# The output projection in seven half-size products, with its sums made on chip

## The chip, the cores and the metric

The kernel runs on one core of a Trainium2 chip. The metric is device time in microseconds (us) of one execution, from the first to the last instruction and what lies around them. The engines are TensorE (PE for its matmuls, PEld for its weight loads), VectorE (DVE), ScalarE (ACT), GpSimd (POOL) and SyncE (SP, whose queue issues all DMAs here). They run side by side, each through its own list of instructions in order, and wait for each other by semaphores.

## The reference

A decoder layer with two attention mixers, A (block-sparse) and B (compressed, selected and windowed), over 512 tokens of 1024 channels. What follows the attention is what the change touches:

```python
y_a = o_a * jax.nn.silu(z_a)
y_b = o_b * jax.nn.silu(z_b)
g_m = jax.nn.sigmoid(gate_m)
merged = g_m[..., :D_MODEL] * (y_a @ w_branch_a[l]) + g_m[..., D_MODEL:] * (y_b @ w_branch_b[l])
x = x + merged @ w_out[l]
```

`gate_m` is a part of `rms_norm(x) @ w_in`; everything is float32.

## The kernel before

**Precision.** PE multiplies a rounded format, so every operand is split into a high half (a cast) and a low half (the operand minus its high half). A product is three matmuls: high x high, low x high, high x low (`mm3`, L416). For weights the raw tile `wr` comes from memory, `wh` (L337, mostly ACT, sometimes POOL) and `wl` (L341, mostly DVE) are its halves; `NW` = 8 of each are kept, and `NRAW` = 5 raw tiles.

**Stages.** First the projections, with the attention woven between them on PE; then the gates of mixer A (`gmgate`, tile `pgc`); then the eight branch products of A (`branch(0, j)`, tile `pbr`, 12 matmuls of 512 columns each); then, for j = 0 to 3, the gates of B for channel tiles j and j + 4 together (`gate_pair`, tile `pgw`) and the branch products `branch(1, j)` and `branch(1, j + 4)`; then the output (`last`, tile `po`).

**Gate pairs in seven products.** A pair of gate tiles is a 2 x 2 block product (two halves of the tokens, two channel tiles, two halves of the 8 k tiles). `gate_pair` makes it from seven products of half size instead of eight (Winograd's form of Strassen's scheme), each of 12 matmuls of 256 columns. It needs sums of the weights (`ws`, L378, made on the way in: `s1 = a21 + a22`, `s2 = s1 - a11`, `s4 = a12 - s2`, `s3 = a11 - a21`) and sums of the inputs, made once for all pairs in `x_again` (rows `xa`, `ta`, `tb`, `T`, `th`, `hl`). The products run in the order 1, 5, 6, 3, 7, 2, 4 and use two banks of PSUM pool `g`; sums over products are made by ACT copies (`cu`, `c5`) and DVE additions (L1352 to L1364).

**Merging.** When a branch product is done, DVE multiplies it with its gate (L1382, "gm<-gm,pbr"), adds mixer A's part (L1447, "gm<-gm,gm"), ACT casts the high half `mh` (L1450), DVE or POOL makes the low half `ml` (L1451).

**Output.** Four column groups of 256, in each four row tiles of 128 tokens; every `po` tile is 8 k x 3 = 24 matmuls of 256 columns: 384 in all. An eviction on DVE (L1552) adds a `po` tile to the input rows `xr`, and SP writes it.

**What sets the order.** A planner in the kernel walks the work with its own estimates of durations and writes each engine's list; what stands here are its lists. Tiles named `gm`, `mh`, `ml`, `xa` and the like share `NATT` = 40 attention buffers; a tile that takes the slot of an older one waits until that was last read. PSUM banks: 2 `g`, 2 `s`, 3 `t`, 1 `o`; `s`, `t` and `o` are the attention's.

A path for the output in seven products is in the kernel (`WOUT`, `last_wino`, `m_sums`), and is not used.

Of the kernel before, what the change touches and what calls it, by code (L numbers as in the profile page):

```python
# [19 lines left out]
D = 1024  # L20
# [69 lines left out]
def hybrid_kernel(ctx: ExitStack, tc: tile.TileContext, x, x0, xT, wtok, wchan, gains, w1,  # L90
# [1185 lines left out]
    def x_again():  # L1276
# [4 lines left out]
        T3 = [alloc("T", "T3", dt=F32R) for _ in range(2)]  # L1281
        pools = [alloc("ph", "T1", dt=F32R) for _ in range(3)] + [sp.tile([P, S], F32R, name=nm("T2"), tag="pl", bufs=3) for _ in range(3)]
        for k in range(4):
# [16 lines left out]
            c.do(either(256), lambda e, x1=x1, x2=x2, tb=tb: e.tensor_sub(tb[:, h[0]], x2[:, h[1]], x1[:, h[1]]))  # L1300
            c.do(either(256), lambda e, x2=x2, ta=ta, tb=tb: e.tensor_sub(tb[:, h[1]], x2[:, h[0]], ta[:, h[1]]))
            for n_, (hi, lo) in enumerate((dst[0][0], dst[0][1])):
# [3 lines left out]
                TX[n_ + 1, k] = hi, lo, None  # L1306
            hi, lo = hl_[1], hl_[2]
            c.do({"A": ca(512)}, lambda e, tb=tb, hi=hi: e.copy(hi, tb))
            c.do(either(512), lambda e, tb=tb, hi=hi, lo=lo: e.tensor_sub(lo, tb, hi.bitcast(F32)))
            for n_ in range(2):  # L1310
                TX[n_ + 3, k] = hi[:, h[n_]], lo[:, h[n_]], None
            c.mark(("T", k))
            c2.call(lambda c=c, c1=c1, c2=c2: c.start(max(c1.t, c2.t)))

    def gate_pair(w, j):
        t1, t2 = att("gm", F32), att("gm", F32)
        yield need(*(("T", k) for k in range(4)))
# [25 lines left out]
        c1 = act("a", "c1", h[0])  # L1343
        yield from run(5, "b", True)
# [7 lines left out]
        c12 = Chain(now[0] + 230).do({"D": cd(256)}, lambda e: e.tensor_add(t1[:, h[1]], b["u2"], ps["b"][:, :256]), lambda: ps["b"])  # L1352
# [3 lines left out]
        yield c12.ready  # L1356
        yield from run(2, "c", True)
        c = Chain(now[0] + 230).do({"D": cd(256)}, lambda e: e.tensor_add(t1[:, h[0]], b["c1"], ps["c"][:, :256]),
                                   lambda: ps["c"]).call(lambda: release(b["u"], c.t))
        c.do(either(512), lambda e: e.tensor_mul(t1, t1, R))  # L1360
        gms[w, j] = t1, c.do({"A": ca(512)}, lambda e: e.activation(t1, t1, AF.Tanh, scale=0.5))
# [3 lines left out]
        d.do(either(256), lambda e: e.tensor_mul(t2[:, h[1]], t2[:, h[1]], R[:, h[1]]))  # L1365
        gms[w, j + 4] = t2, d.do({"A": ca(512)}, lambda e: e.activation(t2, t2, AF.Tanh, scale=0.5))

    def branch(w, j):
# [6 lines left out]
        for c in mm3(ps, ws, [yhl["ab"[w], k] for k in range(4)]):  # L1375
# [5 lines left out]
        yield gc.ready  # L1381
        return Chain(max(now[0] + 230, gc.t)).do({"D": 602}, lambda e: e.scalar_tensor_tensor(  # L1382
            g, g, 1.0, ps, op0=ALU.add, op1=ALU.mult), ps)
# [16 lines left out]
    def gemms():  # L1400
# [32 lines left out]
        for j in (0, 4, 1, 5, 2, 6, 3, 7):  # L1433
            if not WGATES:
                yield from gmgate(1, j)
            elif j < 4:
                yield from gate_pair(1, j)
# [7 lines left out]
            ch = yield from branch(1, j)  # L1445
            g0, g1, a, b = gms[0, j][0], gms[1, j][0], att("mh"), att("ml")
            ch.do(either(512), lambda e, g0=g0, g1=g1: e.tensor_add(g0, g0, g1))  # L1447
            fs[j] = g0, ch.mark(("m", j))
            w_ = 256 if WOUT and j < 4 else 512
            ch.do({"A": ca(w_)}, lambda e, g0=g0, a=a, w_=w_: e.copy(a[:, :w_], g0[:, :w_]))  # L1450
            ch.do(either(w_), lambda e, g0=g0, a=a, b=b, w_=w_: e.tensor_sub(b[:, :w_], g0[:, :w_], a[:, :w_].bitcast(F32)))  # L1451
            ms[j] = a, b, ch
            if WOUT and j >= 4:
                m_sums(j - 4, fs)
# [28 lines left out]
    def last_wino(ms, xr):  # L1483
# [26 lines left out]
        rest = ((5, "b", True), (6, "a", False), (3, "b", False), (7, "a", False), (2, "c", True), (4, "a", False))  # L1510
        for c, p_, z_, first in [(c, 1, "a", True) for c in range(2)] + [(c, *z) for c in range(2) for z in rest]:
            ws = W.take(2, 256)
            for t in range(2):
# [156 lines left out]
```

## Time and profile before

| | us |
|---|---|
| median of 3 runs | 480.58 (480.02 to 481.2) |
| the profiled execution | 479.89 |
| its span, first to last instruction | 478.1 |

The granted TensorE clock is 1.0 throughout. Some lines of the profile are shown in the prediction. There L416 is `mm3`'s line, so matmuls are told apart by their tile. A group's mean duration of a matmul (281 ns for 256 columns) is longer than the distance between two of them, since matmuls overlap in the array.

### The profile page before, as it was taken

How to read it: one execution, taken by the hardware profiler on the slowest of the kernel's cores; microseconds unless marked ns; L12 is line 12 of the kernel's file. 1: busy time of each engine (PE TensorE's matmuls, PEld its weight loads, DVE VectorE, ACT ScalarE, POOL GpSimd, SP SyncE). 2: the span in 40 equal slices, each digit the busy share in tenths (PEclk: the TensorE clock that was granted, in tenths of full speed). 3: DMA queues.
4: the chain of work that ended last, by engine and by line, in shares of the span. 5: the costliest groups of instructions: out<-in, count | busy, mean ns of one | idle time of the engine just before them, and what ended most of it. 6: DMA issues, size and time to landing. Idle time of an engine off the chain costs nothing.

```text
span 478.1 us, 9136 instructions
## 1 busy us (share of the span) xinstructions
PE 468.5 (98%) x3220; PEld 429.2 (90%) x3220; DVE 368.2 (77%) x920; ACT 282.5 (59%) x683; POOL 166.9 (35%) x218
## 2 busy tenths in 40 slices
PE   9999999999999999999999999999989999999997
PEld 8999898999999989888888888888868899889997
DVE  6888988788898489897778768786698789875331
ACT  8666594587787276677776568676654455533200
POOL 1266492077764033554442045346031101100000
PEclk9999999999999999999999999999999999999999
DMA  8835234443433313222212222211821243285421
GB/s 303 239 101 155 69 108 114 136 134 114 110 102 119 111 45 111 54 60 68 63 47 72 83 67 66 69 44 48 275 59 61 90 133 106 59 257 185 145 67 44
DMA packets 29053, 51.30 MB, mean 107 GB/s; under 512 B 3216, under 2 KB 5648, under 8 KB 29008
## 3 DMA queue, kind: packets, MB, share of 16 engines
q1 hardware_dynamic: 29008, 50.73, 35.5%
q8 instruction: 25, 0.41, 0.4%
q14 instruction: 20, 0.16, 0.1%
HBM read 47.96 MB, written 2.75 MB: 106 GB/s over the span
## 4 chain that ended last, share of the span: by engine, by line
PE 82%; DVE 10%; ACT 3%; issue 2%; DMA 2%; SPq 0%; ACTq 0%; DVEq 0%
PE pgc L416 21%; PE pgt L416 18%; PE po L416 9%; PE pgw L416 7%; PE O L1035 6%; PE pt L1001 5%; PE sps L954 3%; PE sps L955 3%; PE pbr L416 3%; DVE wl L341 3%; PE pq L886 2%; DVE ws L378 1%; ACT wh L337 1%; DVE gm L1382 1%; ACT xa L1288 1%
## 5 line engine op out<-in xcount | busy, mean ns | idle before, releaser
L341 DVE TENSOR_TENSOR wl<-wr,wh 128x512 fp32r<-128x512 f32 (+1 forms) x113 | 79.1, 704 | 5.6 <-ACT wh L337 5.1
L416 PE MATMUL pgt<-wh,hh 128*128 128x256 f32 (+1 forms) x288 | 82.6, 287 | 0.4 <-DVE X L772 0.4
L416 PE MATMUL pgt<-wl,hh 128*128 128x256 f32 (+1 forms) x288 | 81.6, 283 | 0.2 <-DVE wl L341 0.2
L416 PE MATMUL pgt<-wh,hl 128*128 128x256 f32 (+1 forms) x288 | 81.1, 281 | 0.0
L337 ACT CAST wh<-wr 128x512 fp32r<-128x512 f32 (+1 forms) x94 | 57.2, 619 | 18.2 <-DMA wr<-in_wout 12.9
L992 POOL TENSOR_SCALAR P<-P,sst,gate 128x512 f32<-128x512 f32 (+3 forms) x56 | 40.2, 722 | 62.7 <-DVE sst L991 58.5
L973 DVE CUSTOM_DVE_ANT_0 sb<-sps,T 128x512 f32<-128x512 f32 (+3 forms) x96 | 46.0, 485 | 20.0 <-PE sps L955 18.5
L416 PE MATMUL pgc<-hh,wh 128*128 128x512 f32 x144 | 59.5, 414 | 0.0
L416 PE MATMUL pgc<-hl,wh 128*128 128x512 f32 x144 | 56.8, 395 | 0.0
L416 PE MATMUL pgc<-hh,wl 128*128 128x512 f32 x144 | 56.8, 394 | 0.0
L988 ACT ACTIVATE P<-sb,sst 128x512 f32<-128x512 f32 (+3 forms) x88 | 50.9, 579 | 8.0 <-DVE sst L973 7.3
L416 PEld LDWEIGHTS pgt<-wh,hh 128*128 128x128 f32 x288 | 54.3, 188 | 1.2 <-PE sps L955 0.6
L416 PEld LDWEIGHTS pgt<-wl,hh 128*128 128x128 f32 x288 | 54.2, 188 | 0.6 <-DVE wl L341 0.4
L416 PEld LDWEIGHTS pgt<-wh,hl 128*128 128x128 f32 x288 | 54.3, 188 | 0.4
L1013 ACT CAST ph<-pt 128x512 fp32r<-128x512 f32 (+2 forms) x72 | 33.5, 479 | 26.5 <-PE pt L1001 25.9
L1001 PE MATMUL pt<-cst,P 128*128 128x128 f32 x232 | 40.6, 272 | 0.0
L1015 DVE TENSOR_TENSOR pl<-pt,ph 128x512 fp32r<-128x512 f32 (+2 forms) x72 | 38.5, 549 | 2.0 <-ACT ph L1013 1.7
L458 POOL TENSOR_TENSOR nr<-nss,mhalf 128x4 f32<-128x4 f32 x28 | 30.7, 1099 | 16.3 <-DVE nss L457 15.8
L416 PE MATMUL po<-wh,mh 128*128 128x256 f32 x128 | 36.0, 281 | 0.2 <-DVE xr L1552 0.2
L416 PE MATMUL po<-wh,ml 128*128 128x256 f32 x128 | 35.9, 281 | 0.2 <-DVE ml L1451 0.2
L416 PE MATMUL po<-wl,mh 128*128 128x256 f32 x128 | 35.9, 280 | 0.0
L992 POOL TENSOR_SCALAR P<-P,sst 128x512 f32<-128x512 f32 (+3 forms) x32 | 21.6, 679 | 32.9 <-DVE sst L991 31.8
(266 smaller groups left out, 1270.4 us busy)
## 6 DMA issues: line engine op xcount, KB each, us to landing
wr<-in_wchan SPq DMA_DIRECT2D x52, 256.0 KB, 2.8
wr<-in_wtok SPq DMA_DIRECT2D x36, 256.0 KB, 2.9
T<-rtab SPq DMA_DIRECT2D x16, 256.0 KB, 3.8
wr<-in_w SPq DMA_DIRECT2D x16, 256.0 KB, 2.8
wr<-in_wbr SPq DMA_DIRECT2D x16, 256.0 KB, 2.7
wr<-in_wout SPq DMA_DIRECT2D x16, 256.0 KB, 3.0
xr<-in_x SPq DMA_DIRECT2D x8, 256.0 KB, 5.4
out_y<-xr SPq DMA_DIRECT2D x16, 128.0 KB, 1.7
```

Of the source, the lines that this page charges most:

```text
L337: e.copy(hi, raw())
L341: c.do(either(n), lambda e: e.tensor_sub(lo, raw(), hi.bitcast(F32))).mark((w, 1, i))
L416: nc.tensor.matmul(dst, sts[i][a], mvs[i][b], start=(start and i == a == b == 0), stop=(stop and i == n - 1 and b == 1), skip_group_check= ...
L458: c.do({"p": 430 + 150 * w}, lambda e: e.tensor_tensor(v(dst), v(ss), mhalf[:parts, :w], op=ALU.pow))
L954: nc.tensor.matmul(sps[:, :n], qs[:, b * P:(b + 1) * P], ks[:, :n], start=True, stop=False)
L973: e.tensor_tensor_reduce(z["sb"][:, :L], sps[:, :L], T[:, S - L:], scale=-1.0, scalar=3e38, op0=ALU.add, op1=ALU.min, accum_out=st[:, 0, b ...
L988: e.activation(pv(), z["sb"][:, :L], AF.Exp, bias=st[:, 0, b:b + 1], scale=-1.0, accum_out=st[:, 1, b:b + 1])
L992: c.do({"P": 315 + 0.834 * L}, lambda e: e.tensor_scalar(pv(), pv(), st[:, 2, b:b + 1], g, op0=ALU.mult, op1=ALU.mult))
L1001: nc.tensor.transpose(pt[:, (b - kb) * P:(b - kb + 1) * P], u.p0 if u.p0 is not None and b == 0 else u.pb[:, POFF[b] + kb * P:POFF[b] + (k ...
L1013: e.copy(z["w"][0], pt[:, :w])
L1015: ch.do({"D": cd(w)}, lambda e: e.tensor_sub(z["w"][1], pt[:, :w], z["w"][0].bitcast(F32)), pt)
L1035: nc.tensor.matmul(O[0][:, S - n:], v.bitcast(F32) if kb == 3 else v, w, start=(u.first and kb == 0 and i == 0), stop=(u.last and kb == 3 ...
```

## The change

The output is made with `last_wino`: for each of two column groups c, the 2 x 2 block product of rows (tokens 0 to 255 and 256 to 511), k halves and column groups c and c + 2 is made from seven products, each of 2 row tiles x 4 k x 3 matmuls of 256 columns. Products 1 and 2 take w_out and the merged branches as they are; they run first, for both c. The other five take sums of w_out (`ws`, eight per c) and, three of them, sums of merged branches, which `m_sums` makes on chip for each pair as soon as it is merged. Each `po` tile is evicted after every product into the rows that it belongs to, 28 evictions in all; the banks are those of all four PSUM pools.

In the gate pairs product 2, which takes the weights `a12` unsummed, is moved from the sixth to the second place; the banks are now the attention's `s` and `t`; the branch product of j runs between products 7 and 4; the waits for the tanh of a gate are no longer in PE's order. A sum for `x_again`'s second half runs in a chain of its own. One more raw tile is kept (`NRAW` 6), one attention buffer fewer (`NATT` 39).

```diff
-NATT = 40
+NATT = 39
 NW = 8
-NRAW = 5
+NRAW = 6
 WGATES = True
-WOUT = False
+WOUT = True
...
-            tiles.append(Group([a11, a21, a22, a12], [
-                0, ("+", 1, 2, "s1", "sb"), ("-", "s1", 0, "s2", "sb"), ("-", 3, "s2", "s4", "sb"),
-                ("-", 0, 1, "s3", "sb"), 3, 2]))
-            tiles += [(wbr[j + i, 1], 512) for i in (0, 4)]
+            tiles.append(Group([a11, a12, a21, a22, (wbr[j, 1], 512)], [
+                0, 1, ("+", 2, 3, "s1", "sb"), ("-", "s1", 0, "s2", "sb"), ("-", 1, "s2", "s4", "sb"),
+                ("-", 0, 2, "s3", "sb"), 4, 3]))
+            tiles.append((wbr[j + 4, 1], 512))
...
-            c = Chain(held=True)
+            c, d = Chain(held=True), Chain(held=True)
...
-                yield room("g")
-                ps[z_] = psum("g", "pgw")
+                yield room(dict(a="s", b="t", c="t")[z_])
+                ps[z_] = psum(dict(a="s", b="t", c="t")[z_], "pgw")
...
         yield from run(1, "a", True)
         c1 = act("a", "c1", h[0])
+        yield from run(2, "c", True)
...
         yield from run(5, "b", True)
...
         yield from run(7, "a", False)
         c22 = Chain(now[0] + 230).do({"D": cd(256)}, lambda e: e.tensor_add(t2[:, h[1]], b["c5"], ps["a"][:, :256]),
                                      lambda: b["v"])
-        yield c12.ready
-        yield from run(2, "c", True)
...
+        yield from between()
         yield c22.ready
         yield from run(4, "a", False)
...
-        yield gc.ready
-        return Chain(max(now[0] + 230, gc.t)).do({"D": 602}, lambda e: e.scalar_tensor_tensor(
-            g, g, 1.0, ps, op0=ALU.add, op1=ALU.mult), ps)
+        ch = Chain(held=True)
+        gc.call(lambda t=now[0] + 230: ch.start(max(t, gc.t)))
+        return ch.do({"D": 602}, lambda e: e.scalar_tensor_tensor(g, g, 1.0, ps, op0=ALU.add, op1=ALU.mult), ps)
...
+        def merge(j):
+            ch = yield from branch(1, j)
...
+            if WOUT and j >= 4:
+                m_sums(j - 4, fs)
+
+        for j in range(4):
+            if WGATES:
+                yield from gate_pair(1, j, lambda j=j: merge(j))
...
+            yield from merge(j + 4)
         yield from (last_wino if WOUT else last)(ms, xr)
...
-        rest = ((5, "b", True), (6, "a", False), (3, "b", False), (7, "a", False), (2, "c", True), (4, "a", False))
-        for c, p_, z_, first in [(c, 1, "a", True) for c in range(2)] + [(c, *z) for c in range(2) for z in rest]:
+        rest = ((5, "b", True), (6, "a", False), (3, "b", False), (7, "a", False), (4, "a", False))
+        for c, p_, z_, first in ([(c, *z) for z in ((1, "a", True), (2, "c", True)) for c in range(2)] +
+                                 [(c, *z) for c in range(2) for z in rest]):
```

The sums of merged branches (unchanged text, now in use; `x1` and `x2` are the merged tiles k and k + 4, `h` the two halves of the tokens):

```python
c.do(either(256), lambda e: e.tensor_add(ta[:, h[0]], x1[:, h[1]], x2[:, h[1]]))
c.do(either(256), lambda e: e.tensor_sub(ta[:, h[1]], ta[:, h[0]], x1[:, h[0]]))
c.call(lambda: d.start(c.t))
d.do(either(256), lambda e: e.tensor_sub(tb[:, h[0]], x1[:, h[0]], x1[:, h[1]]))
d.do(either(256), lambda e: e.tensor_sub(tb[:, h[1]], x2[:, h[0]], ta[:, h[1]]))
for q, (z, hi, lo) in zip((c, d), ts):
    q.do({"A": ca(512)}, lambda e, z=z, hi=hi: e.copy(hi, z))
    q.do(either(512), lambda e, z=z, hi=hi, lo=lo: e.tensor_sub(lo, z, hi.bitcast(F32)))
```

On DVE, around the start of the last branch product, before (gm_5932 and pbr_6110 belong to the last merged tile):

```order
L341 TENSOR_TENSOR wl_6100<-wr_6028,wh_6099 128x512 [waits DMAHW2_49,Activation_49]
L1382 SCALAR_TENSOR_TENSOR gm_5931<-gm_5931,pbr_6083 128x512 [waits PE_49]
L341 TENSOR_TENSOR wl_6107<-wr_6044,wh_6106 128x512 [waits DMAHW3_49,Activation_49]
L1447 TENSOR_TENSOR gm_4356<-gm_4356,gm_5931 128x512 [waits DVE_49]
L1382 SCALAR_TENSOR_TENSOR gm_5932<-gm_5932,pbr_6110 128x512 [waits PE_49]
L1451 TENSOR_TENSOR ml_6109<-gm_4356,mh_6108 128x512 [waits Activation_49,Pool_49]
```

The same place after (pgw_5969 is the last gate product, pbr_6153 the last branch product, ma and mb the sums of merged branches):

```order
L1488 TENSOR_TENSOR ml_5962<-ma_5959,mh_5961 128x512 [waits PE_49,Activation_49]
L1485 TENSOR_TENSOR mb_5960<-gm_4870,ma_5959 128x256
L1392 SCALAR_TENSOR_TENSOR gm_5965<-gm_5965,pbr_6099 128x512 [waits Activation_49]
L341 TENSOR_TENSOR wl_6124<-wr_6027,wh_6123 128x512 [waits DMAHW2_49,Activation_49]
L341 TENSOR_TENSOR wl_6128<-wr_6070,wh_6127 128x512 [waits DMAHW3_49,Pool_49]
L1445 TENSOR_TENSOR gm_4358<-gm_4358,gm_5965 128x512 [waits DVE_49]
L1370 TENSOR_TENSOR gm_5966<-pgw_5969,R 128x256 [waits PE_49]
L1488 TENSOR_TENSOR ml_5964<-mb_5960,mh_5963 128x512 [waits Activation_49]
L1371 TENSOR_TENSOR gm_5966<-gm_5966,R 128x256
L1449 TENSOR_TENSOR ml_6126<-gm_4358,mh_6125 128x256 [waits PE_49,Activation_49]
```

The sums of the third pair and a gate's last product now stand ahead of the merged low half (ml_6126 for ml_6109). The wait of ml_5962 for PE is for its buffer: the tile th_5123, which the last gate product reads, had it.

On DVE in the output, before: an eviction and a low half in turn.

```order
L341 TENSOR_TENSOR wl_6245<-wr_6126,wh_6244 128x512
L1552 SCALAR_TENSOR_TENSOR xr_6080<-po_6246,xr_6080 128x256
L341 TENSOR_TENSOR wl_6278<-wr_6165,wh_6277 128x512
L1552 SCALAR_TENSOR_TENSOR xr_6077<-po_6279,xr_6077 128x256
L341 TENSOR_TENSOR wl_6311<-wr_6225,wh_6310 128x512
```

After, up to the first halves of summed weights, wl_6283 and wl_6285, which the ninth output tile takes:

```order
L1488 TENSOR_TENSOR ml_6185<-mb_6181,mh_6184 128x512
L378 TENSOR_TENSOR ws_6342<-wr_6280,wr_6255 128x512
L1519 SCALAR_TENSOR_TENSOR xr_6147<-po_6327,xr_6147 128x256
L378 TENSOR_TENSOR ws_6354<-wr_6300,ws_6332 128x512
L341 TENSOR_TENSOR wl_6283<-ws_6332,wh_6282 128x512
L1519 SCALAR_TENSOR_TENSOR xr_6147<-po_6348,xr_6147 128x256
L378 TENSOR_TENSOR ws_6377<-wr_6323,ws_6342 128x512
L341 TENSOR_TENSOR wl_6285<-ws_6342,wh_6284 128x512
```

Between two evictions there are now sums of weights and of merged branches beside the low halves.

More of the change, by code (lines that the diff above doesn't have):

```diff
@@ L585, in hybrid_kernel @@
     if WOUT:
-        tiles += [q(c, i) for c in range(2) for i in range(2)]
+        tiles += [q(c, 2 * z + i) for z in range(2) for c in range(2) for i in range(2)]
         for c in range(2):
@@ L1271, in hybrid_kernel @@
     TX = {}
+    TXheld = []
     def xrows(k):
@@ L1305, in x_again, with gate_pair @@
                 c.do(either(256), lambda e, z=z, hi=hi, lo=lo: e.tensor_sub(lo, z, hi.bitcast(F32)))
-                TX[n_ + 1, k] = hi, lo, None
+                TX[n_ + 1, k] = hi, lo, c
             hi, lo = hl_[1], hl_[2]
-            c.do({"A": ca(512)}, lambda e, tb=tb, hi=hi: e.copy(hi, tb))
-            c.do(either(512), lambda e, tb=tb, hi=hi, lo=lo: e.tensor_sub(lo, tb, hi.bitcast(F32)))
+            d.do({"A": ca(512)}, lambda e, tb=tb, hi=hi: e.copy(hi, tb))
+            d.do(either(512), lambda e, tb=tb, hi=hi, lo=lo: e.tensor_sub(lo, tb, hi.bitcast(F32)))
             for n_ in range(2):
-                TX[n_ + 3, k] = hi[:, h[n_]], lo[:, h[n_]], None
-            c.mark(("T", k))
+                TX[n_ + 3, k] = hi[:, h[n_]], lo[:, h[n_]], d
             c2.call(lambda c=c, c1=c1, c2=c2: c.start(max(c1.t, c2.t)))
-    def gate_pair(w, j):
+    def gate_pair(w, j, between):
         t1, t2 = att("gm", F32), att("gm", F32)
-        yield need(*(("T", k) for k in range(4)))
         h = (slice(0, 256), slice(256, 512))
@@ L1343, in gate_pair @@
         c1 = act("a", "c1", h[0])
+        yield from run(2, "c", True)
+        c = Chain(held=True)
+        c1.call(lambda t=now[0] + 230: c.start(max(t, c1.t)))
+        c.do({"D": cd(256)}, lambda e: e.tensor_add(t1[:, h[0]], b["c1"], ps["c"][:, :256]), lambda: ps["c"])
         yield from run(5, "b", True)
@@ L1351, in gate_pair @@
         yield u2.ready
-        c12 = Chain(now[0] + 230).do({"D": cd(256)}, lambda e: e.tensor_add(t1[:, h[1]], b["u2"], ps["b"][:, :256]), lambda: ps["b"])
+        t = now[0] + 230
+        c.call(lambda: setattr(c, "t", max(c.t, t)))
+        c.do({"D": cd(256)}, lambda e: e.tensor_add(t1[:, h[1]], b["u2"], ps["b"][:, :256]), lambda: ps["b"])
+        c.call(lambda: release(b["u"], c.t))
+        c.do(either(512), lambda e: e.tensor_mul(t1, t1, R))
+        gms[w, j] = t1, c.do({"A": ca(512)}, lambda e: e.activation(t1, t1, AF.Tanh, scale=0.5))
         yield from run(7, "a", False)
@@ L1365, in gate_pair @@
         d.do(either(256), lambda e: e.tensor_mul(t2[:, h[1]], t2[:, h[1]], R[:, h[1]]))
+        if j == 3:
+            for t in TXheld:
+                release(t)
         gms[w, j + 4] = t2, d.do({"A": ca(512)}, lambda e: e.activation(t2, t2, AF.Tanh, scale=0.5))
@@ L1432, in gemms @@
         ms = [None] * 8
-        for j in (0, 4, 1, 5, 2, 6, 3, 7):
-            if not WGATES:
+        def merge(j):
+            ch = yield from branch(1, j)
+            g0, g1, a, b = gms[0, j][0], gms[1, j][0], att("mh"), att("ml")
+            ch.do(either(512), lambda e: e.tensor_add(g0, g0, g1))
+            fs[j] = g0, ch.mark(("m", j))
+            w_ = 256 if WOUT and j < 4 else 512
+            ch.do({"A": ca(w_)}, lambda e: e.copy(a[:, :w_], g0[:, :w_]))
+            ch.do(either(w_), lambda e: e.tensor_sub(b[:, :w_], g0[:, :w_], a[:, :w_].bitcast(F32)))
+            ms[j] = a, b, ch
+            if WOUT and j >= 4:
[3 more added lines that the diff above has]
+                yield from gate_pair(1, j, lambda j=j: merge(j))
+            else:
                 yield from gmgate(1, j)
-            elif j < 4:
-                yield from gate_pair(1, j)
+                yield from merge(j)
+                yield from gmgate(1, j + 4)
             if j == 3:
@@ L1444, in gemms @@
                         dma(xr[t + i, 0], x[(t + i) * P:(t + i + 1) * P, :512], 2048)
[L1445 to L1454, printed above, removed]
+            yield from merge(j + 4)
         yield from (last_wino if WOUT else last)(ms, xr)
```

19 lines of the change are left out of this document (9 added, 10 removed).

## The prediction

> **What bounds the kernel now.** I read the page's busy shares first, then a table of the stages, then the chain that ended last, then the waits of the engine on it.
>
> ```profile
> span 478.1 us, 9136 instructions
> PE 468.5 (98%) x3220; PEld 429.2 (90%) x3220; DVE 368.2 (77%) x920; ACT 282.5 (59%) x683; POOL 166.9 (35%) x218
> PE 82%; DVE 10%; ACT 3%; issue 2%; DMA 2%; SPq 0%; ACTq 0%; DVEq 0%
> ```
>
> PE carries the chain with 82%, but DVE has 10% of it, so somewhere PE waits for DVE. The stages show where. The columns are the stretch, its length, and the busy time (count) of PE, PEld, DVE, ACT, POOL, then granted clock, DMA share and GB/s. The stretches are: all up to the first branch product, the eight branch products of mixer A, the four gate pairs up to the last branch product, from there to the last matmul, and the end.
>
> ```profile
> 0.00:340.41 340.41, 337.14 (x2309) 307.95 (x2309) 273.61 (x752) 227.71 (x579) 153.06 (x207) 1.00 0.35 104
> 340.41:364.25 23.84, 22.50 (x98) 17.88 (x97) 23.17 (x44) 15.06 (x30) 7.13 (x6) 1.00 0.33 102
> 364.25:426.03 61.78, 60.30 (x422) 55.90 (x421) 51.93 (x92) 31.84 (x61) 5.50 (x4) 1.00 0.37 109
> 426.03:475.00 48.97, 48.56 (x396) 47.42 (x394) 19.05 (x36) 7.87 (x13) 1.18 (x1) 1.00 0.42 136
> 475.00:478.10 3.10, 0.00 (x0) 0.00 (x0) 0.42 (x1) 0.00 (x0) 0.00 (x0) 1.00 0.12 42
> 382.35:398.39 16.04, 15.70 (x109) 14.46 (x109) 13.95 (x25) 8.31 (x17) 1.55 (x2) 1.00 0.32 99
> ```
>
> In the gate stage PE is busy 60.30 of 61.78 us and DVE 51.93. One pair (last row) takes 16.04 us for 15.70 us of PE. In the output stage PE is nearly dense and DVE has 30 us free. The chain of one pair and the last stretch:
>
> ```profile
> 382.35 8.70 PE pgw L416 x72
> 391.06 2.80 PE pbr L416 x12
> ...
> 393.94 0.69 DVE gm L1382
> 394.63 0.60 DVE ws L378
> 395.23 0.60 DVE wl L341
> 395.84 0.60 DVE gm L1447
> 396.44 0.60 DVE wl L341
> 397.04 0.61 DVE ws L378
> ...
> 397.75 0.63 ACT wh L337
> 398.39 8.77 PE pgw L416 x72
> ...
> 435.08 39.90 PE po L416 x336
> 475.00 0.42 DVE xr L1552
> ```
>
> Each pair closes a loop: after the first branch product five DVE steps and a cast on ACT make the summed weights of the second product, and PE arrives 0.34 us before they are ready. At the end 336 output matmuls take 39.90 us, 0.119 us each: a matmul's price on the path is this pitch, not the 281 ns of its group.
>
> **What goes.** The output falls from 384 to 336 matmuls (7 products x 2 column halves x 2 row tiles x 4 k x 3); the changed program indeed has 48 matmul rows fewer on PE. 48 x 0.119 = **5.7 us**, all on the path. The gate pairs have as many matmuls as before. They now run product 2 second, from the unsummed weights a12, so the summed ones are needed 12 matmuls (1.4 us) later than now. The loop misses by 0.34 us, so it should close: four pairs at PE's own 15.70 us put the start of the last branch product (call it T) 4 x 15.70 - 2.78 = 60.0 us behind the first pair, now 61.78: **1.8 us**.
>
> **What comes, and its prices.** The work that replaces the matmuls is DVE's.
>
> ```profile
> 386.23 0.68 DVE L341 TENSOR_TENSOR wl<-wr,wh 128x512 fp32r<-128x512 f32 x1
> 386.96 0.42 DVE L1352 TENSOR_TENSOR gm<-cu,pgw 128x256 f32<-128x256 f32 x1
> 387.30 0.68 DVE L341 TENSOR_TENSOR wl<-wr,wh 128x512 fp32r<-128x512 f32 x1
> 463.64 0.42 DVE L1552 SCALAR_TENSOR_TENSOR xr<-po,xr 128x256 f32<-128x256 f32 x1 [1.78 <-PE po L416]
> 463.98 0.68 DVE L341 TENSOR_TENSOR wl<-wr,wh 128x512 fp32r<-128x512 f32 x1
> ```
>
> From start to start a 256-wide operation and an eviction take 0.34 us (386.96 to 387.30, 463.64 to 463.98), a 512-wide one 0.60 us (the chain's steps). New on DVE are 16 sums of output weights, 12 more low halves and 12 more evictions, and per gate pair four 256-wide and two 512-wide steps for the sums of merged branches: 16 x 0.60 + 12 x 0.60 + 12 x 0.34 + 16 x 0.34 + 8 x 0.60 = 31 us, less what POOL takes. The eight more casts of m-sums and twelve of weights go to ACT, which is busy 7.87 of 48.97 us in the output stage: covered. Eight more 256 KB weight loads fit too, at 0.42 DMA share. In the order, the loads that a sum waits for stand 1.3 to 2 us ahead of it if they land in 3 us:
>
> ```profile
> wr<-in_wout SPq DMA_DIRECT2D x16, 256.0 KB, 3.0
> ```
>
> SP also issues the output rows between these loads, each waiting for its eviction; one that is 2 us late would be the next stall.
>
> **Gate pairs.** By its new order DVE has 26, 26, 29 and 25 rows in the four pairs, 13.8 + 13.5 + 15.1 + 12.7 = 55.1 us at these prices. POOL adds to it, since the two block each other:
>
> ```profile
> 380.92 0.69 DVE L378 TENSOR_TENSOR ws<-wr,ws 128x512 f32<-128x512 f32 x1
> 381.52 0.68 DVE L1382 SCALAR_TENSOR_TENSOR gm<-gm,pbr 128x512 f32<-128x512 f32 x1
> 382.12 1.18 DVE L378 TENSOR_TENSOR ws<-wr,wr 128x512 f32<-128x512 f32 x1
> 381.14 1.61 POOL L1451 TENSOR_TENSOR ml<-gm,mh 128x512 fp32r<-128x512 f32 x1 [20.28 <-ACT mh L1450]
> ```
>
> During POOL's operation the DVE row with a PSUM operand keeps its 0.60 us, and the next, with two SBUF operands, takes 1.18 instead of 0.68. A POOL row of 512 thus costs DVE 0.5 us when half covered; bounds are 0 and 1.1 (POOL's end, 382.75, less the end of DVE's row at 381.6). After the change POOL has three such rows in the gate stage, three of 256 and two casts; I take 0.5 each for the eight, 4.0 us. 59.1 us of DVE then stand beside 62.8 of PE: it fits, with about 1 us to spare in the third pair, where I followed the queues row by row.
>
> [...]
>
> **Before the pairs** the same rows run in a new order. Now PE waits there twice:
>
> ```profile
> 355.84 0.47 PE L416 MATMUL pbr<-yh,wh 128*128 128x512 f32 x1 [1.34 <-DVE gm L1382]
> 366.26 0.36 PE L416 MATMUL pgw<-hh,wh 128*128 128x256 f32 x1 [0.43 <-ACT wh L337]
> ```
>
> DVE is 97% busy in that stage (23.17 of 23.84). In the new order evictions 4 and 5 of the branch products stand behind the T sums and two POOL rows, so I expect the 1.34 us to come back as about 1.4 us at the next two products: no gain, bounds -1.3 and +1.5. The first 340 us change only by one more load buffer and small shifts; PE idles 3.3 us there (340.41 - 337.14), so bounds are -1.5 and +1.5; I take 0.
>
> **Output, counted from T.** One attention buffer fewer has a price here: the low half ml_5962 gets the slot of a tile that the last gate product still reads, so DVE, with nothing else it may do, waits until 0.15 us before T. Behind it are six rows of 0.60 and four of 0.34 up to ml_6126, which the first output tile needs: done at 4.8. PE would ask for it at 2.78 + 10 x 0.119 = 3.97: wait 0.9. That tile ends at 5.1, seven more of 12 x 0.119 = 1.43 end at 15.1. The ninth is the first with summed weights. It needs the low half wl_6283 at 15.3; DVE has 14 rows of 0.60, 10 of 0.34 and a POOL block of 0.5 up to its end, at 17.1: wait 1.8. The next, wl_6285, is asked for at 17.8 and done at 18.6: wait 0.8. Then DVE needs 30 x 0.60 + 20 x 0.34 = 24.8 us for what PE does in 19 x 1.43 = 27.1, and PE waits only once more, 0.45 us, for an eviction of a bank it adds to again. T to the last matmul: 2.78 + 336 x 0.119 + 3.9 = **46.7**, now 48.97: **2.3 us**. So of 5.7 us some 3.4 are given back.
>
> **Sum.** -1.8 - 2.3 = -4.1 us; the 3.10 us behind the last matmul stay (one eviction, one 128 KB write). The profiled execution took 479.89 us, 1.8 more than its span and 0.7 below the median 480.58. From the median: **476.5 us**, 0.85% faster. A measurement of this kernel tells about 0.3%, 1.44 us, from no change.
>
> **Rivals.**
> - *PE never waits.* If DVE's waits shrink (an earlier POOL share, a slot that is free), gates and output are dense: -1.8 - 5.7 - 0.6 (the output stage's 48.97 less 2.78 and 384 x 0.119) = -8.1, **472.5 us**. For it: 30 us of DVE are free now. Against: the sums start only when the last merged pair exists, right where PE asks. Chance 0.15.
> - *DVE governs the gates.* DVE's waits in the gate stage are now:
>
> ```profile
> DVE gm L1382 <- PE pbr L416: 4.0, 3, 1.4
> DVE wl L341 <- ACT wh L337: 1.9, 2, 1.2
> DVE gm L1358 <- PE pgw L416: 1.6, 4, 0.4
> DVE gm L1354 <- PE pgw L416: 1.3, 4, 0.3
> DVE gm L1352 <- PE pgw L416: 0.7, 1, 0.7
> ```
>
>  9.5 us in all. If they all stay, because DVE's queue is strictly in order, and the three 512-wide POOL rows cost 1.1 each, the pairs take 55.1 + 3.3 + 2.5 + 9.5 = 70.4 us instead of 64.6 (61.78 + 2.78): +5.8, with the output's -2.3 **484.1 us**. It turns slower once more than 6.0 of the 9.5 us remain (64.6 + 2.3 - 60.9), and measurably so from 7.4. For it: 94% of PE's time is then on DVE. Against: an engine that runs late finds PE's results ready. Chance 0.12.
> - *Gain lost in part*: two thirds of those waits remain (6.3 us: +2.6 - 2.3, 480.9 us), or the first 340 us lose 1.5 and the summed tiles 1 more (479 us). **479.1 to 482 us**, chance 0.16.
> - *The change doesn't do what it says* is excluded: the matmul rows are gone from PE's order.
>
> **How the numbers follow.** The forecast (474.5 to 479) has 0.57. Faster by over 0.3% (below 479.1): the forecast and the dense case, 0.72; the same 0.16; slower 0.12. The range 473.0 to 481.6 leaves out half of the dense and two thirds of the slower case, and takes in -1.5 and +1.5 of the unknown stretches.
>
> **What would show it.** Right: in the new profile the stretch of four pairs takes 62.8 us with PE waits under 0.2 us each; from the start of the last branch product to the last matmul 46 to 47.5 us; PE waits for "DVE ml", then for "DVE wl" twice at the first summed output tile, 3 to 4 us in all; the count of po matmuls is 336. Wrong: PE waits for DVE or ACT in each pair; PE waits on wr from in_wout; a first stretch longer or shorter by over 1.5 us; or no wait at the summed tiles at all.

## The result, and the profile after

The kernel after takes **475.61 us** (median of 4 runs, 475.35 to 477.15), the kernel before beside it 480.4 (4 runs, 480.02 to 481.2): ratio 0.9905, 95% interval 0.988 to 0.993. The prediction was 476.5, in a range of 473.0 to 481.6. The profiled execution took 475.35 us, its span is 473.4 us, 4.7 less than before. Five of ten runs of the kernel after had a mean granted clock of 0.995 to 0.996 and took 476.5 to 477.65 us, while the other five and all 51 runs of the kernel before beside the experiments had 0.999 or 1.0 (the five took 475.25 to 475.79), so medians "at full clock" below are those of runs with at least 0.999.

The page of the kernel after, its span, its busy shares and its chain:

```profile
span 473.4 us, 9154 instructions
PE 463.6 (98%) x3172; PEld 424.5 (90%) x3172; DVE 399.2 (84%) x994; ACT 288.8 (61%) x693; POOL 171.8 (36%) x218
PE 80%; DVE 13%; ACT 2%; issue 2%; POOL 2%; POOLq 0%; DVEq 0%
```

48 matmuls are gone, PE is 4.9 us less busy, DVE 31.0 us more (399.2 against 368.2), and DVE's share of the chain has grown from 10% to 13%. The same stages as before the change, columns as there:

```profile
0.00:340.84 340.84, 337.74 (x2308) 308.81 (x2309) 277.93 (x767) 224.41 (x571) 146.17 (x200) 1.00 0.36 105
340.84:364.21 23.37, 22.58 (x97) 17.89 (x96) 22.72 (x43) 14.86 (x29) 9.38 (x7) 1.00 0.28 93
364.21:423.53 59.32, 59.32 (x421) 55.55 (x420) 54.95 (x101) 32.69 (x64) 13.66 (x9) 1.00 0.38 117
423.53:470.26 46.73, 43.93 (x350) 42.28 (x348) 43.19 (x86) 16.86 (x29) 2.55 (x2) 1.00 0.55 175
470.26:473.40 3.14, 0.00 (x0) 0.00 (x0) 0.42 (x1) 0.00 (x0) 0.00 (x0) 1.00 0.20 70
```

Stage by stage the change brought +0.4, -0.5, **-2.5** (gate pairs), **-2.2** (output) and 0 us, -4.7 in all. In the gate stage PE is busy in every one of the 59.32 us; in the output it is idle for 2.8 us while DVE works 43.19 of 46.73. The chain of the kernel after, start and length, shows the same: PE alone through the four pairs (the first of them shown), then almost only DVE from 425.60 until PE's last 132 matmuls.

```profile
364.38 8.52 PE pgw L416 x72
372.90 2.78 PE pbr L416 x12
375.68 1.41 PE pgw L416 x12
377.09 2.77 PE pbr L416 x12
379.86 8.53 PE pgw L416 x72
...
425.60 0.68 DVE wl L341
...
453.34 0.60 DVE ws L378
454.33 15.91 PE po L416 x132
```

A pair now takes 379.86 - 364.38 = 15.48 us, and nothing of it is a wait. The three waits of PE in the output, in its timeline (start, length, line, operands, idle before and releaser), and the two places of DVE's timeline from which the first comes:

```profile
428.54 0.39 PE L416 MATMUL po<-wh,ml 128*128 128x256 f32 x1 [0.73 <-DVE ml L1449]
440.50 0.39 PE L416 MATMUL po<-wl,mh 128*128 128x256 f32 x1 [1.29 <-DVE wl L341]
442.04 0.39 PE L416 MATMUL po<-wl,mh 128*128 128x256 f32 x1 [0.56 <-DVE wl L341]
```

```profile
420.94 0.76 DVE L1362 TENSOR_TENSOR gm<-gm,R 128x512 f32<-128x512 f32 x1
423.45 0.69 DVE L1488 TENSOR_TENSOR ml<-ma,mh 128x512 fp32r<-128x512 f32 x1 [1.75 <-PE pgw L416]
...
428.07 0.42 DVE L1449 TENSOR_TENSOR ml<-gm,mh 128x256 fp32r<-128x256 f32 x1
```

DVE stands still for 1.75 us for the slot that the last gate product (PE pgw) still reads, then works without a pause, and the row that the first output tile needs ends at 428.49. From there to 442 us DVE has no pause either, so the two low halves `wl` wait for their turn in its queue.

### The profile page after: what moved, and what is told of

Read it like the earlier page. It is cut to its first block, busy times and chain, and to the rows that moved or that the text cites. A ratio compares the mean times of both kernels' runs of the same rounds, so it can differ in the third digit from the quotient of the medians.

```text
span 473.4 us, 9154 instructions
## 1 busy us (share of the span) xinstructions
PE 463.6 (98%) x3172; PEld 424.5 (90%) x3172; DVE 399.2 (84%) x994; ACT 288.8 (61%) x693; POOL 171.8 (36%) x218
## 4 chain that ended last, share of the span: by engine, by line
PE 80%; DVE 13%; ACT 2%; issue 2%; POOL 2%; POOLq 0%; DVEq 0%
PE pgc L416 19%; PE pgt L416 18%; PE pgw L416 8%; PE O L1035 6%; PE pbr L416 6%; PE pt L1001 5%; DVE wl L341 4%; PE po L416 3%; PE sps L954 3%; PE sps L955 3%; PE pgf L631 3%; DVE ws L378 1%; DVE xr L1519 1%; PE pq L886 1%; PE pw L475 1%
## 5 line engine op out<-in xcount | busy, mean ns | idle before, releaser
L341 DVE TENSOR_TENSOR wl<-wr,wh 128x512 fp32r<-128x512 f32 (+1 forms) x108 | 75.3, 703 | 4.4 <-ACT wh L337 3.9
L337 ACT CAST wh<-wr 128x512 fp32r<-128x512 f32 (+1 forms) x81 | 49.4, 616 | 0.4 <-DMA wr<-in_wtok 0.2
L992 POOL TENSOR_SCALAR P<-P,sst 128x512 f32<-128x512 f32 (+3 forms) x32 | 24.9, 782 | 44.3 <-DVE sst L991 37.8
L458 POOL TENSOR_TENSOR nr<-nss,mhalf 128x4 f32<-128x4 f32 x28 | 29.5, 1057 | 24.6 <-DVE nss L457 24.2
L416 PE MATMUL po<-wl,mh 128*128 128x256 f32 x112 | 31.7, 283 | 1.9 <-DVE wl L341 1.9
L1001 PEld LDWEIGHTS pt<-cst,P 128*128 128x128 f32 x232 | 29.0, 140 | 4.5 <-POOL P L992 1.0
L416 PEld LDWEIGHTS pgc<-hl,wh 128*128 128x128 f32 x144 | 27.0, 188 | 6.4
```

Source lines behind the costliest of these rows:

```text
L337: e.copy(hi, raw())
L341: c.do(either(n), lambda e: e.tensor_sub(lo, raw(), hi.bitcast(F32))).mark((w, 1, i))
L416: nc.tensor.matmul(dst, sts[i][a], mvs[i][b], start=(start and i == a == b == 0), stop=(stop and i == n - 1 and b == 1), skip_group_check= ...
L458: c.do({"p": 430 + 150 * w}, lambda e: e.tensor_tensor(v(dst), v(ss), mhalf[:parts, :w], op=ALU.pow))
L992: c.do({"P": 315 + 0.834 * L}, lambda e: e.tensor_scalar(pv(), pv(), st[:, 2, b:b + 1], g, op0=ALU.mult, op1=ALU.mult))
L1001: nc.tensor.transpose(pt[:, (b - kb) * P:(b - kb + 1) * P], u.p0 if u.p0 is not None and b == 0 else u.pb[:, POFF[b] + kb * P:POFF[b] + (k ...
```

## The experiments

Two lengths are given for each kernel, both from the starts of PE's rows in its timeline: "gates" from the first gate product to the first output product, "output" from there to the end of the last matmul. "PE's gaps" is what the distances between the 336 output matmuls add up to above 0.1175 us each. The kernel after was run again beside the last three: its lengths repeat within 0.03 us, its start of the gates within 0.04. Each ratio is to runs of the kernel before taken beside it: their median is 480.06 us for gates alone, output alone, product 2 back and old banks, 479.83 for slot free, no weight sums, branch back and product 3 first, and 480.19 for the others.

| kernel | median (runs) | at full clock | gates | output | PE's gaps |
|---|---|---|---|---|---|
| before | 480.06 (23) | 480.06 | 64.38 | 46.33 | |
| after | 475.61 (4) | 475.42 (of both) | 62.10 | 43.91 | 4.27 |
| after, again | 476.88 (6) | as above | 62.08 | 43.90 | 4.26 |
| gates alone | 477.68 (5) | 477.68 | 61.99 | 46.05 | |
| output alone | 480.05 (11) | 480.05 | 67.83 | 42.22 | 2.58 |
| product 2 back | 479.56 (11) | 479.0 (2 runs) | 62.94 | 46.48 | 6.84 |
| old banks | 482.38 (6) | none | 72.45 | 41.85 | 2.21 |
| slot free (40 buffers) | 474.79 (5) | 474.47 | 62.08 | 42.63 | 2.99 |
| no weight sums | 473.0 (5) | 473.0 | 62.05 | 40.94 | 1.30 |
| branch back, 40 | 479.95 (12) | 479.95 | 68.59 | 42.04 | 2.40 |
| product 3 first, 40 | 473.87 (4) | 473.87 | 62.08 | 41.97 | 2.33 |
| product 2 back, 40 | 475.58 (5) | 475.54 | 62.92 | 43.10 | 3.46 |
| product 3 first, other banks, 40 | 476.22 (5) | 475.61 | 62.08 | 44.09 | 4.45 |
| GpSimd kept out, 40 | 475.2 (4) | 475.2 | 62.38 | 43.21 | 3.57 |

**The two halves apart.** First the gates alone:

```diff
-WOUT = True
+WOUT = False
```

> The kernel after with the old output stage: the whole product with w_out in 384 matmuls, no sums of merged branches; gate pairs, banks and load buffers are those of the kernel after. My theory: the gain is the sum of two parts that add. The gate part alone keeps its 2.5 us: pairs at 15.5 us each, from the first gate product to the last branch product about 59.3 us, the output stage as in the kernel before (49.0 us from the last branch product to the last matmul), 0.4 us later up to the pairs: about 478.0 us, ratio 0.995. Rival (the two parts need each other: it is the sums or the sixth load buffer's use in the output that pays): the gates alone bring less than 1 us, 479.4 us or more.

Measured 477.68 us, ratio 0.9945 (0.9933 to 0.9957); gates 61.99 us. PE waits for nothing in the pairs or at the start of the output. Then the output alone: the kernel before with `WOUT = True`, `NATT = 39`, `NRAW = 6` and the new order and banks of the output's products, but its own `gate_pair` and order of branch products.

> The kernel before with the seven half-size output products, the sums of merged branches, 39 attention buffers and 6 load buffers; gate pairs in their old order and old banks. My theory: the output part keeps about 2.3 us (46.7 us from the last branch product to the last matmul), but the sums of merged branches (about 10 us more of VectorE in the gate stage) now stand in the loop that PE already missed by 0.34 us in each pair, so the gates get longer by 1 to 3 us: 479 to 481 us, little or no gain. Rival (the new order of the gates is not needed for the output's gain): gates unchanged at 61.8 us, 478.1 us.

Measured 480.05 us, ratio 0.9995 (0.9986 to 1.0003): no gain at all. Its waits of PE (total, times, longest):

```profile
PE pgw L416 <- ACT wh L337: 2.3, 4, 1.2
PE po L416 <- DVE wl L341: 1.2, 2, 0.6
PE pbr L416 <- DVE gm L1388: 1.0, 2, 0.7
PE pbr L416 <- DVE gm L1361: 0.9, 1, 0.9
```

The output got its 4.1 us (46.33 to 42.22), and the gates gave 3.5 back. In the profiled execution the pairs also begin 1.2 us later (365.47 against 364.25); why stays open. The gates lose at other places than I expected. In pairs two to four PE misses the loop by 0.33 to 0.36 us, about as before. 0.8 us come at the first pair (the wait of 1.2), ahead of the first sum of merged branches at 386.5: a low half on DVE takes 1.71 us of the chain there (365.23), where others take 0.60. The other 2.6 us come at product 4 and at the branch product behind it, 0.9 of them in pairs two and three and 1.7 in the last: there PE waits 0.3 and 0.9 us for additions out of PSUM banks which stand behind rows of these sums in DVE's queue, one of which itself waits 0.9 us for PE. So the two halves do not simply add, as the first expectation said: in gates plus output they bring 2.7 and 0.7 us apart and 4.7 together (in medians 2.4, 0 and 4.8). The new gates are what makes room for the new output.

**What of the gates does it.** Three edits were undone one at a time. First product 2, in the sixth place again, banks and branch product as after:

```diff
         yield from run(1, "a", True)
         c1 = act("a", "c1", h[0])
-        yield from run(2, "c", True)
...
         yield from run(7, "a", False)
...
+        yield c12.ready
+        yield from run(2, "c", True)
...
         yield from between()
```

> The kernel after with one edit undone: the product with the unsummed weights a12 stands in the sixth place of each gate pair again, as in the kernel before; the banks, the branch product between the seventh and the last product, and the output stage stay. My theory: the order closes the loop, so without it PE waits in each pair again, 0.3 us at least and up to 1 us, since VectorE has more to do in the pair than before: 1.4 to 4 us, 477.0 to 479.6 us. Rival (the banks or the moved branch product close the loop): no wait of PE above 0.2 us in the pairs, 475.6 us within 0.5.

Measured 479.56 us, ratio 0.9987 (0.9976 to 0.9997). The time is in the expected span, but not at the expected place. PE's waits from the pairs on, and then the longest wait of DVE:

```profile
PE po L416 <- DVE wl L341: 2.3, 3, 0.9
PE po L416 <- ACT mh L1445: 1.3, 1, 1.3
...
PE po L416 <- DVE ml L1446: 0.6, 1, 0.6
PE pgw L416 <- ACT cu L1342: 0.3, 1, 0.3
```

```profile
DVE ml L1485 <- PE pgw L416: 3.1, 1, 3.1
```

The pairs stay nearly dense (gates +0.8 us, one wait of 0.3 at the last pair). The loss is in the output, +2.6 us: DVE now waits 3.1 us, not 1.75, for the slot, and the rows that end the first half of the pair stand behind that wait. Undoing the banks:

```diff
-                yield room(dict(a="s", b="t", c="t")[z_])
-                ps[z_] = psum(dict(a="s", b="t", c="t")[z_], "pgw")
+                yield room("g")
+                ps[z_] = psum("g", "pgw")
```

> The kernel after with one edit undone: all three sums of a gate pair are in the two banks of the branch products again, not in the attention's; the product with a12 stays in the second place. The third sum of a pair must then wait until VectorE has taken the second out of its bank, for which it needs ScalarE's copy of the first. My theory: this edit is what lets product 2 stand second; without it PE waits once in each pair, 0.23 us for the end of the matmul, 0.42 us for VectorE's add and up to two rows of 0.6 us ahead of it, 0.7 to 1.8 us, in four pairs 2.6 to 7 us: 478.2 to 482.8 us. Rival (the banks do nothing, the order all): 475.6 us within 0.5.

Measured 482.38 us, ratio 1.0048 (1.0033 to 1.0064), slower than before the change and in the range of my theory.

```profile
PE pgw L416 <- DVE gm L1349: 6.4, 4, 1.8
```

PE waits once in each pair, 1.6 us on average, for the bank; three sums held at once need three banks. Not all of the loss is these waits: in two stretches of the profiled execution the granted clock falls, to 0.79 from 384 to 392 us and to 0.83 from 420 to 430 us, which costs 1.7 us each (last section). Last the branch product, behind product 4 again; this kernel has 40 buffers and is held against the one with 40 further below.

```diff
-        yield from between()
         yield c22.ready
         yield from run(4, "a", False)
...
+            if WGATES:
+                yield from merge(j)
             yield from merge(j + 4)
```

> To be held against the kernel after with 40 attention buffers, which it has too: the first branch product of each gate pair stands behind the pair's last gate product again, next to the second one, as in the kernel before; the product with a12 stays in the second place, the banks stay the attention's. In the run with product 2 back in the sixth place the pairs stayed at 15.5 us and the loss came in the output stage, against my expectation. So theory one, new: the branch product between the seventh and the last gate product is what closed the loop in the pairs (VectorE gets the branch product 1.4 us earlier than it gets the gate's last product), and here PE waits in each pair again, 0.3 to 1 us: 1.2 to 4 us above the kernel with 40 buffers. Theory two, that of the prediction: product 2 in the second place is enough by itself: no waits above 0.2 us in the pairs, the same time as with 40 buffers within 0.5 us.

Measured 479.95 us, ratio 1.0001 (0.999 to 1.0012), 5.5 us above the 474.47 at full clock of the kernel with 40 buffers.

```profile
PE pgw L416 <- DVE gm L1365: 5.4, 4, 1.6
PE po L416 <- DVE wl L341: 0.9, 2, 0.5
```

Theory two falls. Theory one has the direction but not the mechanism: no wait for summed weights comes back (no "ACT wh"). PE waits before product 4 for DVE's addition out of the bank that product 7 has just filled. In the kernel before product 2 stood between 7 and 4 and covered that addition; where product 2 leaves, the branch product must take its place.

**What sets the output.** One more buffer; every engine's list stays as it is:

```diff
-NATT = 39
+NATT = 40
```

> The kernel after with 40 attention buffers in place of 39; every engine has the same instructions in the same order, only which buffer a tile lies in changes. In the kernel after VectorE waits 1.75 us for the buffer that the last gate product still reads, just ahead of the last branch product, and from there VectorE is on the chain for 29 us. My theory (VectorE's queue sets the waits of the output stage): with another buffer that wait is gone, the rows behind it start up to 1.75 us earlier, and PE's waits of 0.7, 0.7 and 1.3 us in the output shrink by about as much: 473.9 to 474.9 us, likeliest 474.2. Rival (the waits are set by the merged branches themselves, or by the weights' loads and casts): the wait is gone but PE's waits stay, 475.6 us within 0.4.

Measured 474.79 us, ratio 0.9889 (0.9869 to 0.9908). DVE's timeline at the place of the 1.75 us, then PE's waits:

```profile
421.22 0.68 DVE L1362 TENSOR_TENSOR gm<-gm,R 128x512 f32<-128x512 f32 x1
421.82 0.68 DVE L1488 TENSOR_TENSOR ml<-ma,mh 128x512 fp32r<-128x512 f32 x1
```

```profile
PE po L416 <- DVE wl L341: 1.7, 2, 1.2
PE pbr L416 <- DVE gm L1392: 0.8, 1, 0.8
PE po L416 <- DVE xr L1519: 0.2, 1, 0.2
```

The slot wait is gone, PE's wait for `ml` too, and the gaps are 1.28 us smaller (4.27 to 2.99). The two waits for `wl` stay almost as they were, since PE comes as much earlier as DVE: the gain shows in the time, not in those waits. The medians differ by less than the runs scatter; the traces carry this one. Now the sums of weights are left out, so that this kernel's output is not the layer's:

```diff
-            for f_ in (lambda i: ("-", 2 + i, i, f"t1{i}", ("sb", "ph")[i]),
...
-                outs += [f_(0), f_(1)]
+            for z in (0, 2, 4, 6, 6):
+                outs += [z, z + 1]
```

> The kernel after without the 16 sums of output weights: their products take unsummed weights in their place. All casts, low halves, loads, matmuls and evictions stay. VectorE loses 16 rows of 0.60 us, 9.6 us of its work, and the chain sum - cast - low half of a weight is shorter by one step. My theory (VectorE's queue sets the waits): PE's waits for low halves of weights (0.7 and 1.3 us) go, the wait at the first output tile (0.7 us) may stay, since no sum stands ahead of it: 473.0 to 473.8 us. Rival (loads or ScalarE's casts set them): 475.6 us within 0.4.

Measured 473.0 us, ratio 0.9847 (0.9829 to 0.9864). Both waits for `wl` and the one for an eviction are gone, the one for `ml` stays:

```profile
PE pbr L416 <- DVE gm L1389: 0.8, 1, 0.8
PE po L416 <- DVE ml L1446: 0.7, 1, 0.7
```

With the loads, ScalarE's casts and the matmuls as they were, the rival falls: it is DVE's queue. That the chain of a weight is a step shorter here is no rival, since in the kernel after DVE has no pause ahead of these rows. Then product 3, whose weights are not summed, first:

```diff
+        rest0 = ((3, "e", True), (5, "b", True), (6, "a", False), (7, "a", False), (4, "a", False))
...
-                                 [(c, *z) for c in range(2) for z in rest]):
+                                 [(c, *z) for c in range(2) for z in (rest, rest0)[c == 0]]):
...
+                if c == 0 and p_ in (3, 5):
+                    rd[z_, c, t] = add(c, z_, t, r, half, False, p_ == 3)
+                    if p_ == 5:
+                        rd[z_, c, t] = add(c, z_, t, t, 1, False, True)
+                    continue
```

> The kernel after with 40 attention buffers and, in the first column half of the output, product 3 (whose weights are not summed) ahead of product 5 in two banks of its own; product 5 is then added to two output tiles, so that two more evictions of 0.34 us come on VectorE. All is computed as before. The first product with summed weights is asked for two tiles, 2.9 us, later. My theory (the wait is a matter of when PE asks, since VectorE has time to spare later in the stage): PE's waits for low halves at the first summed tiles, 2.0 us in the kernel after, shrink to under 0.7 us, so 1.3 to 2 us less than with 40 buffers or, if those take the waits away already, within 0.3 us of it: 472.6 to 474 us. Rival (the sums of merged branches that product 3 needs are late instead, or VectorE's total work bounds the stage): no gain over 40 buffers, PE waits for the low halves of merged branches in place of weights.

Measured **473.87 us** (473.16 to 474.29), ratio 0.9868 (0.9849 to 0.9886): faster than both kernels, its slowest run below the fastest of ten runs of the kernel after.

```profile
PE po L416 <- DVE xr L1522: 0.8, 2, 0.5
PE pbr L416 <- DVE gm L1395: 0.8, 1, 0.8
PE po L416 <- DVE wl L341: 0.2, 1, 0.2
```

The waits for `wl` fall from 1.7 to 0.2 us; part comes back as waits for evictions, so against 40 buffers alone the gaps shrink by 0.66 us, half of what I expected at least. Product 2 back with 40 buffers, the edit as above:

> The run with product 2 back in the sixth place, now with 40 attention buffers, to be held against the kernel after with 40 (474.8 us): with 39 its pairs stayed dense, and VectorE waited 3.1 us, not 1.75, for the buffer that the last gate product reads. Theory one: the place of product 2 mattered only through that wait; with the buffer free the loss is gone, 474.8 us within 0.6. Theory two: the place matters by itself, because the rows that end the first half of a gate pair (an add, a multiply, a tanh) become ready 2.8 us later, just ahead of the last branch products, and VectorE's queue then carries them into the output stage: 476 to 478.5 us, PE waits for casts and low halves of merged branches.

Measured 475.58 us, ratio 0.9905 (0.9889 to 0.9922). Neither theory is right alone. Against 39 buffers the gaps fall from 6.84 to 3.46 us, so the slot wait was most of that loss; against the kernel with 40 the gates are 0.84 and the output 0.47 us longer, and that much is the place of product 2 itself. The banks of two tiles exchanged:

```diff
-        tags = {("e", 0): "gg", ("a", 0): "ss", ("a", 1): "tt", ("b", 0): "to", ("c", 0): "to", ("b", 1): "gg", ("c", 1): "gg"}
+        tags = {("e", 0): "to", ("a", 0): "ss", ("a", 1): "tt", ("b", 0): "gg", ("c", 0): "to", ("b", 1): "gg", ("c", 1): "gg"}
```

> The run with product 3 ahead of product 5, with the banks of two tiles exchanged: product 3 of the first column half goes into the two banks that its product 2 leaves, which is evicted two tiles earlier than the other half's, and product 5 takes the other two. In that run PE waited 0.3 us at product 3 for an eviction out of its bank and 0.5 us later for one ahead of product 7. My theory: the first of these goes, the second stays: 0.3 us less, 473.6 us; at five rounds this is at the edge of what can be told. Rival: PE waits for the low half instead, no change, 473.9 us.

A miss: 476.22 us, ratio 0.9915 (0.9897 to 0.9932). DVE's timeline, then PE's:

```profile
446.60 1.77 DVE L378 TENSOR_TENSOR ws<-wr,ws 128x512 f32<-128x512 f32 x1
448.29 1.41 DVE L1522 SCALAR_TENSOR_TENSOR xr<-po,xr 128x256 f32<-128x256 f32 x4
```

```profile
449.51 0.36 PE L416 MATMUL po<-wh,mh 128*128 128x256 f32 x1 [2.21 <-DVE xr L1522]
```

The planner, given other banks, handed a low half and a sum to GpSimd at 443.63 and 446.08; DVE's sum beside them took 1.77 us instead of 0.68, four evictions stood behind it, and PE waited 2.21 us. The 0.3 us at product 3 is gone, as expected, but a wait of 0.57 us for a low half is new. Last, GpSimd kept out of all shared rows from the first pair on:

```diff
     def either(n):
-        return {"d": cd(n), "P": cg(n)}
+        return {"d": cd(n)} if "gates" in done else {"d": cd(n), "P": cg(n)}
...
+        done["gates"] = now[0]
         for j in range(4):
```

> The kernel after with 40 attention buffers, with every row that VectorE and GpSimd may share given to VectorE from the first gate pair on (GpSimd keeps only its casts of weights). It tests the price of a GpSimd row, which the prediction put at 0.5 us of VectorE's time. [...] Theory two: GpSimd is the one that waits, and its rows relieve VectorE by their full length, so VectorE is 2 to 4 us later at the end of the gates: 475.5 to 477.5 us, the waits of PE at the first output tile and at the first summed tile grow.

Measured 475.2 us, ratio 0.9895 (0.9877 to 0.9913), 0.7 us above the kernel with 40 buffers at full clock; gates +0.3, PE's gaps +0.58. The time alone can't tell it (474.8 within 0.5 would be no change), but the trace shows a wait for `ml` at the first output tile again:

```profile
PE po L416 <- DVE wl L341: 1.2, 2, 0.9
...
PE po L416 <- DVE ml L1449: 0.4, 1, 0.4
```

That low half ends 64.0 us behind the first gate product, with 40 buffers alone 63.0. DVE has taken over six rows, 2.8 us at 0.60 and 0.34 each, and is 1.1 us later: the GpSimd rows had relieved it by well under half of that length. The kernel after, again:

> The kernel after unchanged, on the same chip and beside the same runs of the kernel before as the three kernels with 40 buffers, so that differences of 0.2 to 0.4% can be told: 475.6 us within 0.5, ratio 0.9905 within 0.002.

476.88 us (475.25 to 477.65), ratio 0.993 (0.9911 to 0.9949): outside what I expected. At full clock it is 475.41, inside, and the trace repeats the first.

## Why the prediction was right, step by step

- **Gate pairs, -1.8 forecast, -2.5 measured.** The loop closed, as forecast. The size was off in one term: "PE's own 15.70" per pair. That is the busy time of a window that held a wait, and the last matmul ahead of a wait is busy for its whole 281 ns, not its distance of 119. So a wait costs more than the idle time that the trace gives for it: by the starts of PE's rows the four waits of the kernel before, 1.5 us of idle time, cost 0.67, 0.61, 0.58 and 0.58 us, 2.4 in all. The first pair really takes 15.48 us; four such pairs less 2.78 give 59.1, measured 59.32. This 0.7 us is nearly all that the forecast missed: -4.1 against -4.7 in the profiled spans. (The loop has six DVE steps in the lines shown, not five; no term rests on it.) The reason given, product 2 in the second place, is only part of it: with product 2 back the pairs stayed almost dense. It takes the place of product 2, the third bank and the branch product between 7 and 4 together: without the second or the third, PE waits 6.4 or 5.4 us, without the first the rows it delays collide with the slot wait. That the branch product replaces product 2 as the cover of an addition was not in the prediction.
- **DVE in the gates, 59.1 us forecast beside 62.8 of PE.** From the first gate product to the first output product DVE is busy 57.7 of 62.1 us: it fits, as forecast. DVE's rows lose 2.7 us to nine GpSimd rows there (what their durations exceed 0.68 and 0.42), 0.3 each where 0.5 was assumed. The rival "DVE governs the gates" fell because only 2.4 of its 9.5 us of waits remained, fewer than the 6.0 from which it decides; the 1.75 for the slot is new.
- **Before the pairs, 0 forecast, 0.0 measured** (364.25 to 364.21). The 1.34 us wait came back as 0.8 (the `pbr` wait), not 1.4. In all profiles with the new chain of `x_again` that stage takes 23.4 us, in the two with the old one 23.8 and 23.7. The start of the first branch product, +0.4 here, moves by 0.35 us between two kernels with the same lists (340.84 and 340.49), so nothing can be read from it: that it and the -0.5 behind it cancel is luck.
- **Output, -2.3 forecast, -2.2 measured; 46.7 forecast, 46.73 measured.** The slot wait was there, ending 0.08 us ahead of T (0.15 forecast). The low halves ended at 16.9 and 18.5 us behind T (17.1 and 18.6). The idle times of 0.73, 1.29, 0.56 and, for an eviction, 0.18 us cost 1.2, 1.6, 0.8 and 0.5 us by the starts of PE's rows, which is what the forecast counts (0.9, 1.8, 0.8 and 0.45; the first is 0.8 by its own terms). The three for low halves come to 3.6 us, within the "3 to 4 us in all" named as a sign. The distance of two matmuls was 0.1175 us instead of 0.119, 0.5 us less in all; gaps of 4.27 us in place of 3.9 and the last matmul's full length make up for it, so that an agreement within 0.03 us is in part luck. 336 matmuls, as forecast. The run without sums confirms the cause, DVE's queue; the run with 40 buffers prices the slot at 1.28 us, which the prediction had counted but not singled out.
- **Weight loads.** PE reads only the halves `wh` and `wl`, so "PE waits on wr" could not have been seen on PE. But from T to the last matmul no engine waits for a load of `w_out` either, as forecast; the loads land 3.3 us after their issue, where 3 was assumed.

The dense rival (472.6 us by its own terms, since 48.97 - 2.78 - 45.7 is 0.5 and not 0.6) was right on the gates, and fell in the output. Even with a free slot and the summed weights asked for later (40 buffers, product 3 first) the gaps are still 2.33 us.

## What to carry to other kernels

When a change swaps matmuls for work on another engine, ask in which stage that engine gets the work, not whether it has time on average: here the same output change was worth 0.7 us in gates plus output with the old gates and 2.0 with the new ones. When a product moves in an in-order list, look at what it covered at its old place. And a buffer pool that is one tile short need cost nothing until a tile lands in a slot that is read up to the very end of a stage, here by the last gate product; of a wait of 1.75 us on DVE, which has time to spare, PE, which has none, then paid 1.28.

## What the runs showed of the hardware

Two waits of 1.77 us were each followed by some 3.3 us of a lower matmul clock. In the trace of the kernel with the old banks:

```profile
386.51 0.36 PE L416 MATMUL pgw<-hh,wh 128*128 128x256 f32 x1 [1.77 <-DVE gm L1349]
386.70 0.28 PE L416 MATMUL pgw<-hh,wl 128*128 128x256 f32 x1
386.82 0.28 PE L416 MATMUL pgw<-hl,wh 128*128 128x256 f32 x1
386.94 0.38 PE L416 MATMUL pgw<-hh,wh 128*128 128x256 f32 x1
387.12 0.41 PE L416 MATMUL pgw<-hh,wl 128*128 128x256 f32 x1
387.33 0.41 PE L416 MATMUL pgw<-hl,wh 128*128 128x256 f32 x1
```

From 386.94 to about 390.3 the matmuls stand 0.21 us apart instead of 0.12, and the granted clock of the stretch from 384 to 392 us is 0.79 (1.7 us lost). The same follows another wait of 1.77 us at 423.06: from 424.58 to about 427.8 the matmuls stand 0.21 us apart, and the granted clock from 420 to 430 us is 0.83 (1.7 us lost). The length of a wait is not the whole condition: the longest in these gates, 1.81 us at 405.54, has no low behind it (granted clock 1.00 from 400 to 408 us). What decides it is not shown by two lows.

The mean clock of the run with these two lows is 0.993; one alone would make it 0.996, an estimate from the 1.7 us lost and the span of 482.3, and half the runs of the kernel after have 0.995 to 0.996. None of those was profiled, so whether they have such a low, and where, stays open. The 12 runs of the kernel with the branch product back, in whose profiled execution PE has four waits of 0.70 to 1.64 us in the gates, had 0.999 or 1.0. Of the 11 with product 2 back nine had 0.993 to 0.996; the profiled execution, with waits of 0.76, 1.31 and 0.61 us close together, is one of the other two.

One GpSimd row was held up for long beside DVE's rows. A row of 256 elements, 0.73 us in the kernel with 40 buffers, took 3.38 us in the kernel after; its row on GpSimd's timeline, and DVE's rows toward its end:

```profile
416.77 3.38 POOL L1484 TENSOR_TENSOR mb<-gm 128x256 f32<-128x256 f32 x1 [8.21 <-PE pgw L416]
```

```profile
419.13 0.41 DVE L1482 TENSOR_TENSOR ma<-ma,gm 128x256 f32<-128x256 f32 x1
419.46 0.41 DVE L1360 TENSOR_TENSOR gm<-cu,pgw 128x256 f32<-128x256 f32 x1
419.79 0.90 DVE L341 TENSOR_TENSOR wl<-wr,wh 128x512 fp32r<-128x512 f32 x1
```

From 416.98 to 419.46 DVE ran five rows with two SBUF operands at their usual pace, 0.34 and 0.60 us from start to start. It fits that GpSimd could go only at 419.46, beside a row that reads PSUM (`pgw`): 419.46 + 0.73 = 420.19 is its end, 420.15, to within 0.04 us, and it is DVE's next row that is 0.2 us longer (0.90 instead of 0.68). So GpSimd was held up over five rows of DVE here, and in the gates of this kernel a GpSimd row cost DVE 0.3 us (2.7 us for nine), less than the 0.5 assumed.
